# Eight gate blocks summed together in the opening of a decoder layer, x turned by products with a diagonal, second weight parts on VectorE

## The chip, the cores and the metric

The kernel runs on one core of a Trainium2 chip. Its metric is the device time of one execution in microseconds. Three runs of the kernel before gave 785.89, 786.16 and 786.79 us; the median is 786.16 us. One more execution was taken with the hardware profiler, and all lines of a trace below come from it.

## The reference

One layer of a decoder over 512 positions and 1024 channels, everything in float32. Only its beginning matters here:

```python
mod = silu(c) @ ada_w + ada_b                      # c (1, 1024), ada_w (1024, 6144)
sh1, sc1, g1, sh2, sc2, g2 = split(mod, 6)
u = rms_norm(x, mix_pre_g) * (1.0 + sc1) + sh1     # x (512, 1024)
proj = u @ w_in                                    # w_in (1024, 6152)
qk_raw, v, o_pre, gates, glu = split(proj, ...)
a, gt = split(glu, 2)                              # 1024 channels each
y = causal_dwconv(a * sigmoid(gt), cv_dw_w)        # 31 taps
y = silu(layer_norm(y))
```

Behind it stand an mLSTM over four heads (q, k, v from `proj`), an output projection, and a feed-forward part with a short convolution. A row of `mod` is a dot product of a row of `ada_w`'s transpose with `silu(c)`.

## The kernel before

**Numbers in two parts.** A float32 product that must be exact enough is made of three products: each operand is split into a first part (rounded, type `fp32r`, suffix `h` or `hi`) and a second part (what the rounding left, `l` or `lo`). `w_split` (L164) does it for weights: the first part is a copy on ScalarE (ACT) at L170, the second a subtraction at L171, on GpSimd (POOL) unless `eng` says otherwise. `mm3` (L186) issues the three products hi·hi, hi·lo, lo·hi at L188, L189 and L190.

**The gate blocks.** The columns of `w_in` that make `a` and `gt` are cut into 16 blocks of 128 columns, eight pairs. A block's result, 128 channels by 512 positions, fills one bank of PSUM, and is a sum over eight row blocks `k` of 128 channels of `u`. In the opening the first `G0 = 6` blocks (three pairs) are summed side by side, row block after row block, because the row blocks of `u` come one by one; the pairs 3 to 7 follow block by block with weights loaded by `w_load` (L174).

**The opening** (L228 to L344), in which ACT, VectorE (DVE) and POOL keep the order of the program (`in_order`, L70). TensorE (PE) and the load queue of SyncE (SP) keep program order in the whole kernel. Elsewhere a planner places the instructions of ACT, DVE and POOL by priority.

1. x is loaded in four blocks `tt` of 128 positions, each in two halves. The sum of squares of a half is made on ACT (L252) and of the other on DVE (L250); `xs` (L260) adds them and a power on POOL (L261) makes the factor of each position. DVE multiplies x by it in place (L237), and PE turns it with transposes (L232) into banks `xT`, channels on partitions. There are eight such banks `xT0` to `xT7`, but only six are free, so the transposes of 6 and 7 (L271) come when 0 and 1 are copied out by `x_out` (L277, ACT).
2. `silu(c)` is made twice, for SBUF (`cb`, L256) and in place in PSUM (`cps`, L258). `cps` holds two of the eight banks until L346.
3. For each row block `k` (L303): the load of the block's gate weights (L306), its split, the load of the next rows of `ada_w` (1 MB in two DMAs, L225), two dot products on DVE (L319, input `cps`), two small DVE instructions for scale and shift `gsk` (L322, L323), the first part of `u` on ACT (L328), the whole of it on ACT (L330), the second part on POOL (L331; on DVE for `k` = 0), and 18 products of PE. For `k` below 2 the 18 come in three passes over the banks (L338), behind that bank by bank with `mm3`.

The loads have two buffers each: a load of rows of `ada_w` waits until the dot products two blocks earlier are done, a load of gate weights until the split two blocks earlier is done.

**Behind the opening**, `glu_gate` (L350) makes `a * sigmoid(gt)` of a pair from its two banks. The 31 taps of the long convolution (L649 to L661), most of them on DVE at a low priority, need it. Their sums lie in the two banks `cv` (L97), which replace `cps`. The result is first needed by PE in `norm_mean` (L682). Behind the last tap come the dot products of later rows of `ada_w` (L155, with `cb`).

Of the kernel before, what the change touches and what calls it, by code (L numbers as in the profile page):

```python
# [17 lines left out]
P = 128  # L18
D = 1024
T = 512  # L20
# [32 lines left out]
def decoder_layer(ctx, tc, w_glu0, x, c, adaT, vecs, w_glu, w_qko, w_v0, w_v, w_out, w_up, w_down, out):  # L53
# [176 lines left out]

    def turn_x(j, tt):
        PE.transpose(xT_ps[j][:, tt * P : (tt + 1) * P], xn[tt][j // NT][:, j % NT * P : (j % NT + 1) * P], ident)  # L232

    xT_ps = [mmbank(f"xT{j}") if j % 6 < 4 else atbank(f"xT{j}") for j in range(KT)]
    def x_scale(tt, xs):
        for hf in range(2):
            V.tensor_scalar(out=xn[tt][hf], in0=xn[tt][hf], scalar1=xs[:, 1:], scalar2=None, op0=ALU.mult)  # L237
            for i in range(NT if hf == 0 else 2):
                turn_x(NT * hf + i, tt)

    opening = in_order()
    opening.__enter__()
    xss = []
    xjunks = [slot(f"xjunk{hf}") for hf in range(2)]
    for tt in range(NT):
        xsq = small.tile([P, 2], F32, tag="adap", name=f"xsq{tt}")
        for hf in range(2):
            xjunk = xjunks[hf]
            if hf:
                V.scalar_tensor_tensor(out=xjunk, in0=xn[tt][hf], scalar=1.0, in1=xn[tt][hf], op0=ALU.mult, op1=ALU.mult, accum_out=xsq[:, hf:])  # L250
            else:
                S.activation(xjunk, xn[tt][hf], AF.Square, accum_out=xsq[:, :1])  # L252
        if tt:
            x_scale(tt - 1, xss[tt - 1])
        if tt == 1:
            S.activation(cb, cps, AF.Silu)  # L256
        if tt == NT - 1:
            S.activation(cps, cps, AF.Silu)  # L258
        xs = small.tile([P, 2], F32, tag="gsk", name=f"xs{tt}")
        V.tensor_scalar(out=xs[:, :1], in0=xsq[:, :1], scalar1=xsq[:, 1:], scalar2=D * EPS, op0=ALU.add, op1=ALU.add)  # L260
        G.tensor_tensor(out=xs[:, 1:], in0=xs[:, :1], in1=mhalf[:, :1], op=ALU.pow)  # L261
        xss.append(xs)
    x_scale(NT - 1, xss[-1])

# [5 lines left out]
    xr = [slot(f"xr{j}") for j in range(KT)]  # L270
    for j in range(6, KT):  # L271
        for tt in range(NT):
            turn_x(j, tt)

# [19 lines left out]
    glu_ps = {}  # L294
    G0 = 6
    glu_w = {}
# [4 lines left out]

    banks0 = [mmbank(f"glu{i}") if i < 4 else atbank(f"glu{i}") for i in range(G0)]
    for k in range(KT):  # L303
        wk = []
        r = adas.tile([P, D], F32, tag="ada", name=f"wglu0_{k}")
        nc.sync.dma_start(r[:, : G0 * P], w_glu0[k])  # L306
        if k == 0:
            for j in range(3):
                x_out(j, S)
        for a, n in ((0, T), (T, (G0 - 4) * P)):  # L310
            wk.append(w_split(r[:, a : a + n], f"wglu0_{k}_{a}"))
        if k + 1 < KT:
# [4 lines left out]
        for i in range(2):  # L317
            junk = small.tile([P, D], BF16, tag="junk", bufs=1, name=f"junk{k}_{i}")
            V.scalar_tensor_tensor(out=junk, in0=first[k][:, i * D : (i + 1) * D], scalar=1.0, in1=cps, op0=ALU.mult, op1=ALU.mult,  # L319
                                   accum_out=part[:, i : i + 1])  # L320
# [3 lines left out]
        if k == 0:  # L324
            x_out(3, S)
            V.tensor_scalar(out=xr[0], in0=xr[0], scalar1=gsk[:, :1], scalar2=gsk[:, 1:], op0=ALU.mult, op1=ALU.add)
        hi, lo = u[k]
        S.activation(hi, xT_ps[0] if k == 0 else xr[k], AF.Identity, scale=gsk[:, :1], bias=gsk[:, 1:])  # L328
        if k:
            S.activation(xr[k], xr[k], AF.Identity, scale=gsk[:, :1], bias=gsk[:, 1:])  # L330
        (G if k else V).tensor_tensor(out=lo, in0=xr[k], in1=hi.bitcast(F32), op=ALU.subtract)  # L331
        if k == 0:
            for j in (6, 7, 4, 5):
                x_out(j, S)
        if k < 2:
            for a, b in ((0, 0), (1, 0), (0, 1)):
                for i, ps in enumerate(banks0):
                    PE.matmul(ps, blk(wk, i)[a], u[k][b], start=k == 0 and a == b, stop=False)  # L338
# [6 lines left out]
    cspool.__exit__(None, None, None)  # L345
    cvpool.append(ctx.enter_context(tc.tile_pool(name="cvpool", bufs=2, space=PSUM)))  # L346

# [797 lines left out]
def _layout(i):  # L1145
# [9 lines left out]
    def tiles(w, starts, per):  # L1155
# [22 lines left out]
    return {  # L1178
        "w_glu0": c_(np.stack([cols(w_in, a0 + b * D + j * P) for j in range(3) for b in range(2)]).transpose(2, 1, 0, 3).reshape(KT, P, 6 * P)),
        "x": c_(f("x")[0]),  # L1180
# [30 lines left out]
```

## Time and profile before

| | us |
|---|---|
| median of three runs | 786.16 |
| the profiled execution | 785.76 |
| its span, first to last instruction | 784.0 |
| PE busy in it | 762.9 |
| DVE busy | 591.6 |
| ACT busy | 408.1 |
| POOL busy | 383.9 |

A row of the timeline has the start, the duration, the engine, the line, the operation, output<-inputs, and in brackets how long the engine was idle and what ended it. PE is the matmul, PEld its load of weights, which lies beside the products. Busy time of PE includes the depth of its pipeline, so durations of neighbouring products overlap: their pace is the difference of two starts. A row of waits has the waiting engine and line, what it waited for, the sum, the number of times and the longest. A row of windows has, for each stretch, the busy time of each engine with the number of instructions, then the granted clock, the busy share of the DMA engines and their rate in GB/s.

### The profile page before, as it was taken

How to read it: one execution, taken by the hardware profiler on the slowest of the kernel's cores; microseconds unless marked ns; L12 is line 12 of the kernel's file. 1: busy time of each engine (PE TensorE's matmuls, PEld its weight loads, DVE VectorE, ACT ScalarE, POOL GpSimd, SP SyncE). 2: the span in 40 equal slices, each digit the busy share in tenths (PEclk: the TensorE clock that was granted, in tenths of full speed). 3: DMA queues.
4: the chain of work that ended last, by engine and by line, in shares of the span. 5: the costliest groups of instructions: out<-in, count | busy, mean ns of one | idle time of the engine just before them, and what ended most of it. 6: DMA issues, size and time to landing. Idle time of an engine off the chain costs nothing.

```text
span 784.0 us, 10572 instructions
## 1 busy us (share of the span) xinstructions
PE 762.9 (97%) x3683; PEld 636.5 (81%) x3683; DVE 591.6 (75%) x938; ACT 408.1 (52%) x766; POOL 383.9 (49%) x313
## 2 busy tenths in 40 slices
PE   7899999899999999999999999999999999999995
PEld 4678888678978888888888998888888888888884
DVE  6659999999998532565868798666555687698996
ACT  6566437667765544572244445444444444456752
POOL 3689758779779544334661446444544440000001
PEclk9999999999999999999999999999999999999998
DMA  8974213302116422334953763332333321778862
GB/s 292 326 274 145 93 71 108 134 28 107 54 54 234 165 89 104 114 110 155 398 176 124 253 217 135 128 123 81 120 114 128 128 91 58 279 257 259 285 222 107
DMA packets 35977, 124.28 MB, mean 159 GB/s; under 512 B 4146, under 2 KB 5586, under 8 KB 29908
## 3 DMA queue, kind: packets, MB, share of 16 engines
q1 hardware_dynamic: 24084, 95.15, 34.7%
q10 hardware_dynamic: 11840, 28.46, 10.2%
q8 instruction: 29, 0.48, 0.2%
q14 instruction: 24, 0.20, 0.1%
HBM read 112.17 MB, written 11.42 MB: 158 GB/s over the span
## 4 chain that ended last, share of the span: by engine, by line
PE 72%; DVE 17%; DMA 4%; ACT 3%; POOL 2%; issue 1%; SPq 0%; DVEq 0%; POOLq 0%; ACTq 0%
PE up L189 10%; PE up L190 10%; PE up L188 10%; DVE cv L661 8%; PE p L190 4%; PE p L189 4%; PE p L188 4%; PE glu L189 3%; DMA wglu<-in_w_glu 2%; PE glu L190 2%; PE glu L188 2%; PE mixa L190 2%; PE mixa L188 2%; PE mixa L189 2%; PE mixb L190 2%; PE mixb L189 2%
## 5 line engine op out<-in xcount | busy, mean ns | idle before, releaser
L661 DVE SCALAR_TENSOR_TENSOR cv<-gt,cvw,cv 128x506 f32<-128x506 f32 (+24 forms) x200 | 134.1, 727 | 0.4
L617 POOL TENSOR_TENSOR ro0r<-ro0t,mhalf 128x1 f32<-128x1 f32 x1 | 0.9, 926 | 125.9 <-DVE ro0t L615 125.9
L171 POOL TENSOR_TENSOR wup_1024l<-wup,wup_1024h 128x512 fp32r<-128x512 f32 x20 | 27.3, 1367 | 31.7 <-ACT wup_1024h L170 31.7
L171 POOL TENSOR_TENSOR wup_0l<-wup,wup_0h 128x512 fp32r<-128x512 f32 x20 | 27.8, 1388 | 29.9 <-ACT wup_0h L170 29.9
L657 POOL TENSOR_TENSOR cs<-cs,cs 128x510 f32<-128x510 f32 (+3 forms) x32 | 41.9, 1308 | 0.2
L171 POOL TENSOR_TENSOR wup_1536l<-wup,wup_1536h 128x512 fp32r<-128x512 f32 x20 | 28.1, 1405 | 27.4 <-ACT wup_1536h L170 27.4
L189 PE MATMUL up<-u2l,wup_0h 128*128 128x512 f32 (+1 forms) x100 | 36.5, 365 | 0.2 <-DVE u2l L830 0.2
L188 PE MATMUL up<-u2h,wup_0h 128*128 128x512 f32 (+1 forms) x100 | 36.6, 366 | 0.0
L188 PE MATMUL up<-u2h,wup_1024h 128*128 128x512 f32 (+1 forms) x100 | 36.5, 365 | 0.0
L190 PE MATMUL up<-u2h,wup_0l 128*128 128x512 f32 (+1 forms) x100 | 36.4, 364 | 0.0
L190 PE MATMUL up<-u2h,wup_512l 128*128 128x512 f32 (+1 forms) x100 | 36.4, 364 | 0.0
L190 PE MATMUL up<-u2h,wup_1536l 128*128 128x512 f32 (+1 forms) x100 | 36.4, 364 | 0.0
L188 PE MATMUL up<-u2h,wup_1536h 128*128 128x512 f32 (+1 forms) x100 | 36.4, 364 | 0.0
L189 PE MATMUL up<-u2l,wup_1024h 128*128 128x512 f32 (+1 forms) x100 | 36.4, 364 | 0.0
L189 PE MATMUL up<-u2l,wup_1536h 128*128 128x512 f32 (+1 forms) x100 | 36.4, 364 | 0.0
L188 PE MATMUL up<-u2h,wup_512h 128*128 128x512 f32 (+1 forms) x100 | 36.4, 364 | 0.0
L189 PE MATMUL up<-u2l,wup_512h 128*128 128x512 f32 (+1 forms) x100 | 36.4, 364 | 0.0
L190 PE MATMUL up<-u2h,wup_1024l 128*128 128x512 f32 (+1 forms) x100 | 36.4, 364 | 0.0
L155 DVE SCALAR_TENSOR_TENSOR junk<-ada,cb 128x1024 bf16<-128x1024 f32 x20 | 31.3, 1565 | 6.4 <-DMA ada<-in_adaT 6.2
L171 POOL TENSOR_TENSOR wup_512l<-wup,wup_512h 128x512 fp32r<-128x512 f32 x20 | 27.2, 1361 | 14.6 <-ACT wup_512h L170 14.6
L655 ACT ACTIVATE cs<-gt,cvw 128x511 f32<-128x511 f32 (+4 forms) x40 | 27.2, 712 | 4.5 <-POOL cs L657 3.8
L171 POOL TENSOR_TENSOR wqko_1024l<-wqko,wqko_1024h 128x512 fp32r<-128x512 f32 x12 | 16.6, 1382 | 22.4 <-PE v L189 12.3
(1061 smaller groups left out, 2685.1 us busy)
## 6 DMA issues: line engine op xcount, KB each, us to landing
wup<-in_w_up SPq DMA_DIRECT2D x22, 1024.0 KB, 7.0
wqko<-in_w_qko SPq DMA_DIRECT2D x12, 1024.0 KB, 5.0
ada<-in_adaT ACTq DMA_DIRECT2D x20, 512.0 KB, 5.9
ada<-in_adaT SPq DMA_DIRECT2D x16, 512.0 KB, 5.9
wo<-in_w_out SPq DMA_DIRECT2D x8, 1024.0 KB, 9.0
spare<-in_adaT ACTq DMA_DIRECT2D x12, 512.0 KB, 7.5
wglu<-in_w_glu SPq DMA_DIRECT2D x5, 1024.0 KB, 8.4
wd<-in_w_down SPq DMA_DIRECT2D x6, 768.0 KB
```

The source lines that it names most:

```text
L155: t = V.scalar_tensor_tensor(out=junk, in0=r, scalar=1.0, in1=cb, op0=ALU.mult, op1=ALU.mult, accum_out=mod[:, i : i + 1])
L171: (eng or G).tensor_tensor(out=lo[:, :n], in0=src, in1=hi[:, :n].bitcast(F32), op=ALU.subtract)
L188: PE.matmul(ps, a[0], b[0], start=start, stop=False)
L189: PE.matmul(ps, a[0], b[1], start=False, stop=False)
L190: PE.matmul(ps, a[1], b[0], start=False, stop=stop)
L617: G.tensor_tensor(out=r, in0=t, in1=mhalf[:, :1], op=ALU.pow)
L655: S.activation(t[:, d:], cvx[j][:, : T - d], AF.Copy, scale=w(CK - 1 - d))
L657: G.tensor_tensor(out=side[:, d:], in0=side[:, d:], in1=t[:, d:], op=ALU.add)
L661: last_tap = V.scalar_tensor_tensor(out=cp[:, d:], in0=cvx[j][:, : T - d], scalar=w(CK - 1 - d), in1=cp[:, d:], op0=ALU.mult, op1=ALU.add)
```

## The change

- The blocks summed together become eight (four pairs). `cps` is given back as soon as `cb` is made, and its two banks become `cv` before the opening, so that `xT` and the gate blocks each have eight banks. The second `silu(c)` goes; the dot products read `cb` in SBUF.
- x is no longer multiplied. DVE multiplies the unit matrix by the factors of the 128 positions (`dg`), and PE multiplies each block of x by this diagonal, which turns and scales in one. It is a full float32 product in place of a transpose.
- A row block's gate weights are 512 KB, loaded in one DMA, where they were 384 KB; in return one load of 1 MB behind the opening goes.
- All second parts in the opening, of the weights and of `u`, are made on DVE. In the program the split now stands behind the dot products.
- Row blocks 0 to 3 go in three passes, the others bank by bank; row block 0 takes the four banks 0 to 3 first.
- For `k` = 0 the whole of `u` is read by DVE from the bank `xT0` itself.

```diff
+    def x_sums(tt):
+        xsq = small.tile([P, 2], F32, tag="adap", name=f"xsq{tt}")
+        S.activation(xjunks[0], xn[tt][0], AF.Square, accum_out=xsq[:, :1])
+        V.scalar_tensor_tensor(out=xjunks[1], in0=xn[tt][1], scalar=1.0, in1=xn[tt][1], op0=ALU.mult, op1=ALU.mult, accum_out=xsq[:, 1:])
         xs = small.tile([P, 2], F32, tag="gsk", name=f"xs{tt}")
         V.tensor_scalar(out=xs[:, :1], in0=xsq[:, :1], scalar1=xsq[:, 1:], scalar2=D * EPS, op0=ALU.add, op1=ALU.add)
         G.tensor_tensor(out=xs[:, 1:], in0=xs[:, :1], in1=mhalf[:, :1], op=ALU.pow)
-        xss.append(xs)
-    x_scale(NT - 1, xss[-1])
+        return xs
+
+    def x_turn(tt, xs):
+        dg = slot(f"dg{tt}")[:, :P]
+        V.tensor_scalar(out=dg, in0=ident, scalar1=xs[:, 1:], scalar2=None, op0=ALU.mult)
+        for j in range(KT):
+            PE.matmul(xT_ps[j][:, tt * P : (tt + 1) * P], xn[tt][j // NT][:, j % NT * P : (j % NT + 1) * P], dg, start=True, stop=True)
+
+    xss = [x_sums(0), x_sums(1)]
+    S.activation(cb, cps, AF.Silu)
+    cspool.__exit__(None, None, None)
+    cvpool.append(ctx.enter_context(tc.tile_pool(name="cvpool", bufs=2, space=PSUM)))
+    xT_ps = [mmbank(f"xT{j}") if j < 4 else atbank(f"xT{j}") if j < 6 else cvbank(f"xT{j}") for j in range(KT)]
+    for tt in range(NT):
+        x_turn(tt, xss[tt])
+        if tt + 2 < NT:
+            xss.append(x_sums(tt + 2))
...
-    G0 = 6
+    G0 = 8
...
+    def passes(wk, k, which):
+        for a, b in ((0, 0), (1, 0), (0, 1)):
+            for i in which:
+                PE.matmul(banks0[i], blk(wk, i)[a], u[k][b], start=k == 0 and a == b, stop=False)
...
         r = adas.tile([P, D], F32, tag="ada", name=f"wglu0_{k}")
-        nc.sync.dma_start(r[:, : G0 * P], w_glu0[k])
-        if k == 0:
-            for j in range(3):
-                x_out(j, S)
-        for a, n in ((0, T), (T, (G0 - 4) * P)):
-            wk.append(w_split(r[:, a : a + n], f"wglu0_{k}_{a}"))
+        nc.sync.dma_start(r, w_glu0[k])
...
-            V.scalar_tensor_tensor(out=junk, in0=first[k][:, i * D : (i + 1) * D], scalar=1.0, in1=cps, op0=ALU.mult, op1=ALU.mult,
+            V.scalar_tensor_tensor(out=junk, in0=first[k][:, i * D : (i + 1) * D], scalar=1.0, in1=cb, op0=ALU.mult, op1=ALU.mult,
                                    accum_out=part[:, i : i + 1])
...
         if k == 0:
-            x_out(3, S)
-            V.tensor_scalar(out=xr[0], in0=xr[0], scalar1=gsk[:, :1], scalar2=gsk[:, 1:], op0=ALU.mult, op1=ALU.add)
+            for j in (1, 2, 3):
+                x_out(j, S)
+        for a in range(0, D, T):
+            wk.append(w_split(r[:, a : a + T], f"wglu0_{k}_{a}", eng=V))
         hi, lo = u[k]
-        S.activation(hi, xT_ps[0] if k == 0 else xr[k], AF.Identity, scale=gsk[:, :1], bias=gsk[:, 1:])
+        src = xr[k] if k else xT_ps[0]
+        S.activation(hi, src, AF.Identity, scale=gsk[:, :1], bias=gsk[:, 1:])
         if k:
-            S.activation(xr[k], xr[k], AF.Identity, scale=gsk[:, :1], bias=gsk[:, 1:])
-        (G if k else V).tensor_tensor(out=lo, in0=xr[k], in1=hi.bitcast(F32), op=ALU.subtract)
+            S.activation(xr[k], src, AF.Identity, scale=gsk[:, :1], bias=gsk[:, 1:])
+        else:
+            V.tensor_scalar(out=xr[k], in0=src, scalar1=gsk[:, :1], scalar2=gsk[:, 1:], op0=ALU.mult, op1=ALU.add)
+        V.tensor_tensor(out=lo, in0=xr[k], in1=hi.bitcast(F32), op=ALU.subtract)
         if k == 0:
-            for j in (6, 7, 4, 5):
+            for j in (4, 5, 6, 7):
                 x_out(j, S)
-        if k < 2:
-            for a, b in ((0, 0), (1, 0), (0, 1)):
-                for i, ps in enumerate(banks0):
-                    PE.matmul(ps, blk(wk, i)[a], u[k][b], start=k == 0 and a == b, stop=False)
+            passes(wk, k, range(4))
+            passes(wk, k, range(4, G0))
+        elif k < 4:
+            passes(wk, k, range(G0))
         else:
             for i, ps in enumerate(banks0):
                 mm3(ps, blk(wk, i), u[k], False, k == KT - 1)
```

More of the change, by code (lines that the diff above doesn't have):

```diff
@@ L229, in decoder_layer @@
     nc.sync.dma_start(vec[:, :FIRST], vecs[:, :FIRST])
[L231 to L239, printed above, removed]
     opening = in_order()
     opening.__enter__()
-    xss = []
     xjunks = [slot(f"xjunk{hf}") for hf in range(2)]
-    for tt in range(NT):
+    def x_sums(tt):
         xsq = small.tile([P, 2], F32, tag="adap", name=f"xsq{tt}")
[L247 to L258, printed above, removed]
+        S.activation(xjunks[0], xn[tt][0], AF.Square, accum_out=xsq[:, :1])
+        V.scalar_tensor_tensor(out=xjunks[1], in0=xn[tt][1], scalar=1.0, in1=xn[tt][1], op0=ALU.mult, op1=ALU.mult, accum_out=xsq[:, 1:])
         xs = small.tile([P, 2], F32, tag="gsk", name=f"xs{tt}")
@@ L300, in glu_weights @@
         glu_w[i] = w_load(w_glu[i], f"wglu{i}")
-    banks0 = [mmbank(f"glu{i}") if i < 4 else atbank(f"glu{i}") for i in range(G0)]
+    banks0 = [mmbank(f"glu{i}") if i < 4 else atbank(f"glu{i}") if i < 6 else cvbank(f"glu{i}") for i in range(G0)]
+    def passes(wk, k, which):
+        for a, b in ((0, 0), (1, 0), (0, 1)):
+            for i in which:
+                PE.matmul(banks0[i], blk(wk, i)[a], u[k][b], start=k == 0 and a == b, stop=False)
     for k in range(KT):
@@ L1178, in _layout @@
     return {
-        "w_glu0": c_(np.stack([cols(w_in, a0 + b * D + j * P) for j in range(3) for b in range(2)]).transpose(2, 1, 0, 3).reshape(KT, P, 6 * P)),
+        "w_glu0": c_(np.stack([cols(w_in, a0 + b * D + j * P) for j in range(4) for b in range(2)]).transpose(2, 1, 0, 3).reshape(KT, P, 8 * P)),
         "x": c_(f("x")[0]),
```

5 lines of the change are left out of this document (removed).

## The prediction

> **What bounds the kernel now.** I read first the windows, then what PE waited for behind the opening.
>
> ```profile
> 20.00:51.30 31.30, 28.17 (x121) 21.74 (x119) 17.96 (x42) 17.24 (x28) 22.44 (x22) 1.00 0.94 332
> 51.30:66.00 14.70, 14.70 (x65) 12.14 (x66) 11.76 (x19) 13.02 (x23) 14.19 (x12) 1.00 0.40 133
> 66.00:150.00 84.00, 84.00 (x424) 71.14 (x423) 80.26 (x131) 45.40 (x80) 68.56 (x58) 1.00 0.33 114
> ```
>
> ```profile
> PE Mb L533 <- DVE Ms L563: 2.4, 1, 2.4
> PE hT L488 <- ACT E L542: 0.4, 1, 0.4
> PE up L189 <- DVE u2l L830: 0.2, 1, 0.2
> ```
>
> From 51.3 us to the tail PE waits three times, 3.0 us in all: PE is the bound there, and an earlier end of the opening should reach the end of the kernel. Between 20 and 51 us the DMA engines are 94% busy at 332 GB/s and PE issues only 121 products, though their pace would allow more:
>
> ```profile
> ACT wglu_0h L170 <- DMA wglu<-in_w_glu: 11.8, 6, 3.3
> DVE junk L319 <- DMA ada<-in_adaT: 9.3, 7, 2.9
> PE glu L189 <- POOL ul L331: 3.1, 3, 1.4
> 65.97 0.39 PE L190 MATMUL glu<-uh,wglu_1536l 128*128 128x512 f32 x1
> 66.19 0.39 PE L188 MATMUL glu<-uh,wglu_0h 128*128 128x512 f32 x1
> 17.20 1.48 PE L338 MATMUL glu<-uh,wglu_0h 128*128 128x512 f32 x4 [0.49 <-ACT uh L328]
> ```
>
> A product takes 0.227 us (65.97 to 66.19). The first is issued at 17.20, and the eighth block ends where the ninth begins, at 66.19: 49.0 us for 192 products that need 192 x 0.227 = 43.6. So **5.4 us of waiting for loads and splits** is what can be won; the change fills it with the fourth pair. The point to follow is this 66.19.
>
> **The turn of x.** It needs the four factors. The last block's square ends at 10.28 on ACT and its power is short:
>
> ```profile
> 9.56 0.63 ACT L252 ACTIVATE xjunk<-xn 128x512 f32<-128x512 f32 x1 [0.72 <-DMA xn<-in_x]
> 10.10 0.18 ACT L252 ACTIVATION_READ_ACCUMULATOR xjunk<-xn 128x1 f32 x1
> 11.67 0.21 DVE L260 TENSOR_SCALAR xs<-xsq 128x1 f32<-128x1 f32 x1
> L261 POOL TENSOR_TENSOR xs<-xs,mhalf x4: 551/924/932, 5.8 to 12.0; 128x1 f32<-128x1 f32 x4
> L237 DVE TENSOR_SCALAR xn<-xn,xs x8: 479/484/487, 6.8 to 12.9; 128x512 f32<-128x512 f32 x8
> ```
>
> Today DVE reaches the last sum at 11.67, behind 0.88 us of scaling per block. With a 128x128 diagonal (between L266's 0.17 and L237's 0.48; I take 0.24, near the small one, since a quarter of L237's elements is left) the sum comes at about 10.4, the power ends at 11.5 to 11.7, the last diagonal at 11.9. The first diagonal is there at about 7.4, where the transposes begin now; PE has work from then on without a gap, and its pace decides:
>
> ```profile
> 15.65 0.23 PEld L232 LDWEIGHTS xT<-ident,xn 128*128 128x128 f32 x1
> 15.86 0.23 PEld L232 LDWEIGHTS xT<-ident,xn 128*128 128x128 f32 x1
> L232 PE MATMUL xT<-ident,xn x32: 417/421/477, 7.3 to 16.3; 128*128 128x128 f32 x32
> L488 PE MATMUL hT<-ident,hn x32: 270/273/329, 211.6 to 363.7; 128*128 128x128 f32 x32
> 333.06 1.06 PE L203 MATMUL ry_b<-ident,ry_r 128*128 128x128 f32 x8
> 333.87 0.48 PE L188 MATMUL mixa<-wo_512h,hh 128*128 128x512 f32 x1
> L139 PE MATMUL cps<-crow,ones x4: 1056/1056/1189, 2.4 to 5.1; 1*128 1x512 f32 x4
> ```
>
> A transpose is one record and a float32 product two (L203: eight records for four products, 0.81 us to the next row, 0.10 each). In the opening records come 0.21 us apart and last 0.42 us, against 0.27 us for L488's later: **PE is at half speed to the end of the transposes**, though the windows say 1.00 there. So a product with the diagonal costs 0.43 us at half speed and 0.20 at full; 32 are 13.8 or 6.4 us. When does the speed rise? After an idle time it is seen once:
>
> ```profile
> 154.16 0.77 PE L533 MATMUL Mb<-Ms,rowsel 128*128 128x512 f32 x1 [2.38 <-DVE Ms L563]
> 154.73 0.63 PE L188 MATMUL qko<-uh,wqko_1024h 128*128 128x512 f32 x1
> 155.16 0.63 PE L189 MATMUL qko<-ul,wqko_1024h 128*128 128x512 f32 x1
> 157.16 0.40 PE L188 MATMUL qko<-uh,wqko_1024h 128*128 128x512 f32 x1
> ```
>
> After 2.4 us of idleness products are 0.43 us apart, and 3.0 us of dense work bring the full pace back; the loss is about 1.3 us. At the start of the program it took longer: transposes with gaps of 0.5 us from 7.3 did it at about 16.5, the four one-row products of L139, dense from 2.4 to 6, not at all. For dense full products from 7.4 I take the rise at 12.0 (4.6 us), between 3.0 us and 9. By then 10.7 products are done; 21.3 x 0.20 = 4.3 us more: the turn ends at 16.3 instead of 16.7, its last eight begin at 14.7.
>
> The Trainium skill, "TensorE: Matmul & The Clock Gate", Part 1, says that the clock is full after a busy window of about 3.4 us that runs freely; by it the rise would fall between 10.8 and 14.2, an estimate that leaves my 12.0 inside. Its Part 4 says that transposes do not count as work for the clock; here the first gate products behind them are at full speed already (L338's weight loads last 0.19 us from 17.2 on), so the trace does not bear that out.
>
> **To the first gate product.**
>
> ```profile
> 13.60 1.57 ACT L277 ACTIVATE xr<-xT 128x512 f32<-128x512 f32 x3 [2.41 <-PE xT L232]
> 15.05 0.64 ACT L170 ACTIVATE wglu_0h<-wglu 128x512 fp32r<-128x512 f32 x1
> L927 DVE TENSOR_TENSOR g2l<-g2kept,g2h 128x512 fp32r<-128x512 f32 x11 | 7.5, 682 | 0.0
> 16.39 0.93 DVE L326 TENSOR_SCALAR xr<-xr,gsk 128x512 f32<-128x512 f32 x1
> ```
>
> On ACT three copies (0.48 each, 13.60 to 15.05) now stand ahead of the first split, and the third bank's turn allows the first at 15.3: split at 16.74, done at 17.37. DVE makes two second parts, which begin at 17.45 and take 0.65 of pace each (0.68 by L927, with POOL idle), and then the whole of `u` for `k` = 0 out of `xT0`, 0.7 to 0.93 (0.7 taken). Block 0's sum uses that bank, so the first gate product waits for this: 18.75 + 0.7 + 0.1 = **19.55**, 2.35 us later than now. PE idles there 3.2 us (16.3 to 19.55), more than the 2.4 that cost the full speed at 154; I take the same 1.3 us loss, between 0 and 1.5. The dot products of block 0, from about 12 with `ada` landed, are done before; the second `silu` that goes (1.0 us of ACT) stood beside transposes and is worth nothing.
>
> **Per row block.** PE needs 24 x 0.227 = 5.45 us.
>
> ```profile
> 18.38 1.21 DVE L319 SCALAR_TENSOR_TENSOR junk<-ada,cps 128x1024 bf16<-128x1024 f32 x1
> 21.09 1.21 DVE L319 SCALAR_TENSOR_TENSOR junk<-ada,cps 128x1024 bf16<-128x1024 f32 x1
> 21.27 0.82 ACT L328 ACTIVATE uh<-xr,gsk 128x512 fp32r<-128x512 f32 x1 [1.35 <-DVE gsk L323]
> 22.12 0.82 ACT L330 ACTIVATE xr<-xr,gsk 128x512 f32<-128x512 f32 x1
> L319 DVE SCALAR_TENSOR_TENSOR junk<-ada,cps x16: 1207/1220/1222, 13.5 to 46.3; 128x1024 bf16<-128x1024 f32 x16
> L155 DVE SCALAR_TENSOR_TENSOR junk<-ada,cb x20: 1209/1438/2318, 235.9 to 471.3; 128x1024 bf16<-128x1024 f32 x20
> ```
>
> DVE: dot products and `gsk` 2.71 (18.38 to 21.09), two second parts to 4.0, then it waits for ACT, which ends the whole of `u` at 0.18 + 1.67 behind `gsk`, 4.56; `ul` to **5.3**. The new wait sits on DVE: the next block's dot products are queued behind `ul`, and with them the release of the `ada` buffers to SP. DMA: 1.57 MB at 332 GB/s is 4.74 us, and a load has about 8 us from its release to its use (two periods less the 2.6 of the dot products). The 1 MB that goes behind the opening stood in a stretch with 40% of DMA and is worth nothing there; nor is the order of the passes, since PE has its operands either way. So the order is PE 5.45, DVE 5.3, DMA 4.74: PE sets the pace, with `ul` of `k` = 0 at 20.1 and of `k` = 7 at 20.1 + 37.1 = 57.2, ahead of its use at 59.0.
>
> The dot products' second input moves from PSUM to SBUF. L155 has that form: 1.21 us at best, 2.3 at worst, in stretches where POOL works. I take 1.22, since POOL has only the factors to make here.
>
> The Trainium skill, "VectorE: DVE Perf Modes", "Two Vector instructions with no wait between them", says that the second SBUF read of VectorE is shared with GpSimd. By it the new form would be the worse one beside a busy POOL; with 2.3 us twice a row block would take 7.5 us. L155's spread fits the rule.
>
> **Sum.** 19.55 + 1.3 + 43.6 = 64.45 against 66.19: **1.7 us won**. The profiled execution (785.76, span 784.0) would be 784.0; it lies 0.4 below the median, and against the median 786.16 I say **784.4**. This is 0.22%, at the edge of what a measurement of this kernel tells from no change (0.2%, 1.6 us).
>
> **What is late next.** All four pairs end together, and the taps' bank is the fourth pair's: the first tap moves from 55.5 to about 66.
>
> ```profile
> L661 DVE SCALAR_TENSOR_TENSOR cv<-gt,cvw,cv x200: 706/726/750, 55.5 to 235.3; 128x502 f32<-128x502 f32 x6, 128x506 f32<-128x506 f32 x5, 128x504 f32<-128x504 f32 x5, 128x489 f32<-128x489 f32 x5
> 311.87 1.02 PE L682 MATMUL ytot<-ysum,ones 128*128 128x512 f32 x2
> ```
>
> DVE did some 15 taps (10 us) by then and is full afterwards, so the last tap goes from 235 to 242 to 246. PE asks for the result at 312: hidden, by 50 us of cover. The dot products of L155 behind it move to 246 to 275.
>
> **Rivals.**
> - *The clock stays down* (slower): products of a diagonal, mostly zeros, raise the speed no better than L139's. The turn ends at 7.4 + 13.8 = 21.2, the first gate product follows at 23.0, the end at 67.9: 787.9. Each us by which the rise comes later costs 0.53 us, so it decides from a rise at about 15.3. For it: nine slow us today. Against it: 3.0 us sufficed at 154. Chance 0.25.
> - *The speed is kept over the gap*, or rises by 10.5: 63.15, or 62.4 with both: 783.1 to 782.4. For it: gaps of 1.3 us cost nothing between 26 and 52. Against it: 154. Chance 0.18.
> - *Given back on DVE*: L155's instructions, 1.2 to 2.3 us each, now stand before `Md` and `E` of the next head, for which PE waits 0.4 us at 266.8 already. One such delay: 785.6 to 786.7; with several on the path 788. Chance 0.16.
> - *The round trip of DVE and ACT, or the larger loads, become the bound*: from 5.56 us per block it shows, at 5.8 nothing is won: 786.1 and above. Against it: the sums above. Chance 0.08.
>
> **Chances.** The forecast itself has 0.33; half of it and a bit lies beyond 0.2%. With the second rival: faster 0.42. The rest of the forecast, part of the first and third: same 0.33. Slower 0.25, mostly the first rival. The range 782.3 to 788.2 reaches from the kept clock to the clock that stays down.
>
> **What would show it.** PE records of the turn falling from 0.21 to 0.10 us apart at about 12; the first L338 successor near 19.5 with products 0.43 apart for some 3 us; dot products of two blocks 5.3 to 5.5 us apart; the ninth block's first product near 64.5; no new wait of PE behind it. Wrong would be a first gate product behind 21.3, DVE waiting for `ada` loads, or a new wait of PE between 240 and 280.

## The result and the profile after

The change makes the kernel **slower**: 789.32 us (787.99 to 789.57, five runs) against 786.10 (785.37 to 786.79, five runs), a ratio of 1.0041 with a 95% interval of 1.0029 to 1.0052. A second set gave 1.0038 (1.0023 to 1.0053). Two executions of over 2700 us, the profiled one of e13 below and one of the kernel before beside e9 to e12, are left out of the ratios, and e13's trace is not read. The profiled execution took 787.99 us, 2.2 more than that of before; its span is 786.2 against 784.0. The trace is of the fastest of the five runs, 1.3 us below their median.

First the opening, in TensorE's timeline of the changed kernel. L250 is the product with the diagonal, L301 the first gate product, L188 at 64.82 the ninth block's first:

```profile
7.73 9.29 PE L250 MATMUL xT<-dg,xn 128*128 128x128 f32 x64 [1.76 <-DVE dg L248]
19.05 1.37 PE L301 MATMUL glu<-uh,wglu_0h 128*128 128x512 f32 x4 [2.02 <-ACT uh L326]
...
64.82 0.39 PE L188 MATMUL glu<-uh,wglu_0h 128*128 128x512 f32 x1
```

The point that the prediction followed stands at 64.82 instead of 66.19: the opening wins 1.37 us. Then what TensorE waits for in the whole kernel (sum, times, longest):

```profile
PE hT L486 <- DVE hn L480: 4.0, 1, 4.0
...
PE glu L301 <- ACT uh L326: 2.0, 1, 2.0
...
PE glu L189 <- DVE ul L331: 1.3, 1, 1.3
PE Mb L531 <- DVE Ms L561: 0.6, 1, 0.6
```

The first row is new. `hT` turns the result of a head and waits for `hn`, its normalized form; this wait is that of head 1. The lead of 1.37 us grows at `Mb` of head 0 (a wait of 0.6 us, and no half clock behind it, where before had 2.4 and the half clock) and is lost at that `hT`. Before, then after, in TensorE's timeline of 250 to 274 us:

```profile
256.89 0.40 PE L533 MATMUL Mb<-Ms,rowsel 128*128 128x512 f32 x1
266.77 0.66 PE L488 MATMUL hT<-ident,hn 128*128 128x128 f32 x4 [0.42 <-ACT E L542]
270.14 1.02 PE L455 MATMUL s<-q_0c,k_2c 128*128 128x512 f32 x2
```

```profile
253.38 0.40 PE L531 MATMUL Mb<-Ms,rowsel 128*128 128x512 f32 x1
266.42 2.03 PE L486 MATMUL hT<-ident,hn 128*128 128x128 f32 x8 [4.02 <-DVE hn L480]
270.81 0.41 PE L188 MATMUL v<-wv_4h,uh 128*128 128x256 f32 x1
271.02 0.33 PE L189 MATMUL v<-wv_4l,uh 128*128 128x256 f32 x1
272.13 0.28 PE L189 MATMUL v<-wv_5l,uh 128*128 128x256 f32 x1
272.25 0.28 PE L190 MATMUL v<-wv_5h,ul 128*128 128x256 f32 x1
272.38 1.02 PE L453 MATMUL s<-q_0c,k_2c 128*128 128x512 f32 x2
```

At `Mb` of head 2 the changed kernel is 3.51 us ahead, at `s` of head 2 2.24 us behind, which is the difference of the spans. Of the 5.75 us, 4.02 are the wait, against 0.42 before; the other 2.15 are lost behind it, mostly because products come 0.21 us apart until 271.0 (270.81 to 271.02) and 0.12 from then on (272.13 to 272.25): the idle time cost the full speed. The windows 262 to 273 show it, before and then after (granted clock third from the end):

```profile
262.00:273.00 11.00, 10.58 (x74) 8.98 (x72) 4.94 (x8) 9.26 (x20) 5.26 (x4) 1.00 0.17 59
```

```profile
262.00:273.00 11.00, 6.98 (x38) 6.38 (x37) 9.83 (x17) 4.38 (x8) 8.16 (x6) 0.69 0.53 179
```

DVE is busy 9.8 of these 11 us where it had been 4.9, and DMA 53% where it had been 17%. The chain of waits of the changed kernel, 250 to 275 us, says with what:

```profile
255.16 0.04 DVE cv L659
...
255.79 1.81 DVE junk L155 x2
...
257.62 0.33 ACTq L153
...
257.98 1.28 ACT L538
...
260.00 3.68 DMA ada<-in_adaT
...
263.77 1.23 DVE junk L155 x2
265.01 1.28 DVE hn L480
```

Behind the last tap (L659, the `cv` row) come dot products of the rows 16 to 23 (L155). Their loads (L153) are issued in ACT's order, each when a dot product has freed one of the two buffers; DVE waits for the load, and `hn` waits behind both, until 265.0. GpSimd had its factor `fac` ready 2.9 us before, at 262.10:

```profile
261.07 1.03 POOL L477 TENSOR_TENSOR fac<-ssq,mhalf 128x4 f32<-128x4 f32 x1
```

In the kernel before the taps had ended 20 us earlier. The taps' group, after (first and last start at the end of the figures):

```profile
L659 DVE SCALAR_TENSOR_TENSOR cv<-gt,cvw,cv x200: 691/726/750, 69.6 to 255.2; 128x483 f32<-128x483 f32 x7, 128x498 f32<-128x498 f32 x5, 128x489 f32<-128x489 f32 x5, 128x487 f32<-128x487 f32 x5
```

### The profile page after: what moved, and what is told of

Read it like the earlier page. It is cut to its first block, busy times and chain, and to the rows that moved or that the text cites. A ratio compares the mean times of both kernels' runs of the same rounds, so it can differ in the third digit from the quotient of the medians.

```text
span 786.2 us, 10624 instructions
## 1 busy us (share of the span) xinstructions
PE 763.6 (97%) x3715; PEld 640.9 (82%) x3715; DVE 606.2 (77%) x957; ACT 406.0 (52%) x760; POOL 353.9 (45%) x286
## 4 chain that ended last, share of the span: by engine, by line
PE 72%; DVE 20%; ACT 3%; DMA 2%; issue 1%; SPq 0%; ACTq 0%; DVEq 0%
PE up L189 10%; PE up L190 10%; PE up L188 10%; DVE cv L659 9%; PE p L189 4%; PE p L190 4%; PE p L188 4%; PE glu L189 2%; PE glu L190 2%; PE glu L188 2%; DVE junk L314 2%; PE mixa L190 2%; PE mixa L188 2%; PE mixa L189 2%; PE mixb L190 2%; PE mixb L189 2%
## 5 line engine op out<-in xcount | busy, mean ns | idle before, releaser
L659 DVE SCALAR_TENSOR_TENSOR cv<-gt,cvw,cv 128x497 f32<-128x497 f32 (+24 forms) x200 | 135.7, 727 | 1.6 <-ACT cv L647 0.9
L188 PE MATMUL up<-u2h,wup_0h 128*128 128x512 f32 (+1 forms) x100 | 36.5, 365 | 0.0
L188 PE MATMUL up<-u2h,wup_1024h 128*128 128x512 f32 (+1 forms) x100 | 36.4, 364 | 0.0
L188 PE MATMUL up<-u2h,wup_512h 128*128 128x512 f32 (+1 forms) x100 | 36.4, 364 | 0.0
L188 PE MATMUL up<-u2h,wup_1536h 128*128 128x512 f32 (+1 forms) x100 | 36.4, 364 | 0.0
L155 DVE SCALAR_TENSOR_TENSOR junk<-ada,cb 128x1024 bf16<-128x1024 f32 x20 | 30.6, 1530 | 7.4 <-DMA ada<-in_adaT 7.3
L170 ACT ACTIVATE wup_1024h<-wup 128x512 fp32r<-128x512 f32 x22 | 13.9, 631 | 25.9 <-PE up L189 20.4
```

Of the source, the lines that this page charges most:

```text
L155: t = V.scalar_tensor_tensor(out=junk, in0=r, scalar=1.0, in1=cb, op0=ALU.mult, op1=ALU.mult, accum_out=mod[:, i : i + 1])
L170: S.activation(hi[:, :n], src, AF.Copy)
L188: PE.matmul(ps, a[0], b[0], start=start, stop=False)
L659: last_tap = V.scalar_tensor_tensor(out=cp[:, d:], in0=cvx[j][:, : T - d], scalar=w(CK - 1 - d), in1=cp[:, d:], op0=ALU.mult, op1=ALU.add)
```

## The experiments

Each ratio is against the kernel before on the same chip; the changed kernel itself was run beside e5 to e7 only, so the other runs are set beside it by their ratios. **Theory**: the four pairs end together, so the taps start and end later; the dot products and loads of rows 16 to 23, which follow the last tap, then stand in front of `hn` of head 1. **Rivals**: GpSimd's backlog makes `hn`'s factor late; or the new opening itself loses the time.

| run | median us | ratio, 95% interval |
|---|---|---|
| the change again | 788.88 | 1.0038 (1.0023 to 1.0053) |
| e1 rows 16 to 23 later | 786.48 | 1.0026 (1.0010 to 1.0042) |
| e2 the same in before | 786.38 | 1.0002 (0.9984 to 1.0021) |
| e3 first split of the fifth pair later | 790.10 | 1.0061 (1.0048 to 1.0074) |
| e4 both | 788.03 | 1.0040 (1.0023 to 1.0058) |
| e5 before, taps later | 788.70 | 1.0038 (1.0023 to 1.0053) |
| e6 eight taps fewer on DVE | 788.22 | 1.0031 (1.0014 to 1.0047) |
| e7 transposes for the diagonal | 786.12 | 1.0003 (0.9986 to 1.0020) |
| e9 loads of rows 16 to 23 on SP | 787.27 | 1.0023 (1.0013 to 1.0032) |
| e10 e7 and e1, loads on SP | 784.93 | 0.9993 (0.9983 to 1.0004) |
| e11 e7, loads on SP | 784.70 | 0.9985 (0.9970 to 1.0001) |
| e12 before, loads on SP | 791.81 | 1.0082 (1.0068 to 1.0096) |
| e13 e7, rows behind head 2 | 811.23 | 1.0318 (1.0300 to 1.0336) |
| e15 the same with the diagonal | 810.29 | 1.0301 (1.0282 to 1.0320) |
| e14 e7, rows before the gates | 801.68 | 1.0211 (1.0190 to 1.0231) |
| e8 before, second parts on DVE | 807.23 | 1.0269 (1.0243 to 1.0296) |
| e16 e7, rows beside the gates | 788.10 | 1.0030 (1.0016 to 1.0045) |
| e17 the same with the diagonal | 788.04 | 1.0032 (1.0015 to 1.0049) |

**The dot products behind another point (e1, e2).**

```diff
     for i in range(16, 24):
-        ada_block(i, last_tap)
+        ada_block(i, los[1])      # head 1's last second part (L492)
```

> The changed kernel with the eight dot products of rows of ada_w behind the last tap (L155, blocks 16 to 23) placed behind the last second part of head 1's attention instead. Theory A (these dot products and their loads stand in front of hn on VectorE and hold PE 4.0 us at hT, and the idle time costs the full clock, 1.3 us more): the wait falls to 0.5 us or less, nothing runs at half speed behind it, and the time goes from 789.3 to 784 to 785. Theory B (the late taps have filled GpSimd, and the factor fac, which ended at 262.1, is late by itself): the wait stays at 1.2 to 2.2 us and the time is 786.5 to 788. If neither is it: 789.

> The same placement in the kernel before, as a control. Theory A: only the 0.4 us wait of PE at hT can go: 785.6 to 786.3, no change clear of noise. If the placement is worth something by itself, without the changed opening: 784 or below.

TensorE's waits in e1:

```profile
PE o L464 <- ACT hn L468: 3.1, 1, 3.1
...
PE hT L486 <- DVE hn L480: 0.5, 1, 0.5
```

The wait at `hT` falls from 4.0 to 0.5 us, so these dot products did stand in its way; but 30 us later, in the same attention step of head 2, ACT comes late with a copy, and TensorE waits 3.1 us. ACT had waited for buffers of L155:

```profile
290.85 0.63 ACT L170 ACTIVATE wv_4h<-wv 128x512 fp32r<-128x512 f32 x1 [2.28 <-DVE junk L155]
```

Then, at 293.62, ACT waited 2.14 us more for `q_1c`, which DVE made late behind such a dot product. So the wait moved. The forecast of 784 to 785 us was missed, though the traced execution, of 784.49 us, lies in it: by the ratios about a third of the loss came back, but the intervals overlap (1.0010 to 1.0042 against 1.0029 to 1.0052). In the kernel before the same edit makes a wait of 2.2 us at `o` and no gain: it is no improvement of its own.

**The hiccup at the end of the opening (e3, e4).** In the changed kernel ACT splits the fifth pair's weights between `uh` and `xr` of row block 7, which makes the 1.3 us at `ul`. e3 moves the call of the fifth pair's `w_load` into the ordered part, behind row block 7; e4 adds e1.

```diff
+    glu_weights(G0 // 2)
     opening.__exit__(None, None, None)
...
-        glu_weights(i)
+        if i > G0 // 2:
+            glu_weights(i)
```

> The changed kernel with the split of the fifth pair's weights kept behind the opening's last instruction on ScalarE (in the changed kernel its first piece, waiting for its load, stands in front of the whole of u of the last row block and holds PE 1.25 us at ul). The ninth block begins 1.3 us earlier, at 63.5. Theory A or B (hn is set by other engines, not by PE): PE then waits at hT longer by as much, and the time stays at 789 (788.5 to 789.5). If PE's lead is kept instead: 788.0.

> Both edits together. Theory A: 782.7 to 784, since the 1.3 us of the opening now reach the end. Theory B: 786 to 787.5, the opening's 1.3 us are lost at hT. Neither: 788 to 789.

The wait at `ul` goes in both, and the time does not: e3's waits at `Mb` and `hT` are 1.8 and 2.8 us (the latter in two). But its ninth block also begins later, at 65.13 instead of the 63.5 expected: TensorE's clock rose later in that run, and the first gate products ran at half speed behind their wait of 2.03 us (last section). In e4 it is 65.51. So neither says what 1.3 us won in the opening would be worth, and e4's 788.03 is the value expected if neither theory holds.

**The change again, and late taps alone (e5).**

> The changed kernel itself, beside the three that follow. Both theories: 1.0030 to 1.0052 of the kernel before, TensorE idle about 4.0 us at hT of head 1 (262 to 266 us), ninth block's first product near 64.8 us. A profile near 789.5 us instead of 788.0 would show one more stretch at half clock; theory: behind the wait at Mb of head 0 (140 to 160 us) or behind the gap at 17 to 20 us.

e5 is the kernel before, whose first taps wait for the fourth pair's gate:

```diff
+            if j < 3 and d == SIDE + 1:
+                tc.add_manual_dep(last_tap.ins, gates[3].ins.name, ...)
```

> The kernel before with one thing alone taken from the changed one: the taps on VectorE begin only behind the fourth pair's gate (near 67 us instead of 55.5). The opening is that of before, so the ninth block's first product stays at 66.2 us. Theory A (late taps push the adaLN dot products of rows 16 to 23 in front of hn): last tap 245 to 250 us instead of 235, TensorE idle 1.5 to 4 us at hT of head 1 near 262 us, time 1 to 4 us above the kernel before. Rival (the new opening itself, its PSUM or its splits, makes the loss): last tap moves, but the wait at hT stays 0 and the time is within 0.7 us of before.

The first taps of the first three pairs wait so. The taps' group in e5, then TensorE at its longest wait behind the opening, and a row of its waits:

```profile
L662 DVE SCALAR_TENSOR_TENSOR cv<-gt,cvw,cv x200: 689/725/750, 67.6 to 253.6; 128x506 f32<-128x506 f32 x6, 128x498 f32<-128x498 f32 x6, 128x504 f32<-128x504 f32 x5, 128x502 f32<-128x502 f32 x5
```

```profile
210.38 1.46 PE L489 MATMUL hT<-ident,hn 128*128 128x128 f32 x8 [2.43 <-DVE hn L483]
```

```profile
PE s L456 <- DVE E L457: 1.4, 2, 1.0
```

With before's opening untouched (its ninth block begins at 66.17), starting the taps 12 us later ends them 18 us later and costs the same 0.4% as the whole change. **So the late taps cost time by themselves, and the new opening is not needed for it.** The place is not the expected one. The wait at `hT` is that of head 0, at 210 us, where DVE does eight taps in a row ahead of `hn`; no dot product of rows 16 to 23 has come by then. At head 1, near 262 us, TensorE does not wait. Behind it those dot products stand in front of `E` of head 2 (the 1.4 us at `s`), as the prediction's third rival said. Two things stay open. The trace is of an execution of 786.64 us, 2.1 below e5's median, and shows a loss of 0.9 us only. And e5 has no wait at `Mb` of head 0 either (TensorE is there at 151.66, before at 154.16): what the changed kernel wins there can come from the late taps alone, without its opening.

**Fewer taps on DVE (e6).** `SIDE = 6`: eight taps go to ACT and POOL.

> The changed kernel with SIDE = 6: one tap in each of eight pairs goes from VectorE (8 x 0.73 us less there) to ScalarE and GpSimd (8 x 1.3 us more there). Theory A (VectorE is late): last tap near 249 us instead of 255, the wait at hT falls from 4.0 to 2 us or less, time 1 to 2 us below the changed kernel on the same chip. Theory B (GpSimd's backlog makes fac late): the wait at hT stays at 4 us or grows, time equal or up to 3 us above the changed kernel.

```profile
PE s L453 <- DVE so L488: 3.2, 1, 3.2
...
PE hT L486 <- DVE hn L480: 0.8, 1, 0.8
```

The last tap starts at 245.0, the wait at `hT` falls to 0.8, as the theory said and GpSimd's rival did not. But `so`, one link further in the same chain, now waits behind a dot product whose load is late, and the time is within the interval of the changed kernel's. The theory had the place right and the gain wrong. `hn` itself now waits 2.2 us for GpSimd's factor (3.7 in e9): that backlog is next in line, at under 1 us for TensorE at head 1, and not the cause.

**Transposes instead of the diagonal (e7).** DVE scales x and TensorE turns it with transposes; banks, order and second parts stay as in the changed kernel.

```diff
-        dg = slot(f"dg{tt}")[:, :P]
-        V.tensor_scalar(out=dg, in0=ident, scalar1=xs[:, 1:], scalar2=None, op0=ALU.mult)
...
+            V.tensor_scalar(out=xn[tt][hf], in0=xn[tt][hf], scalar1=xs[:, 1:], scalar2=None, op0=ALU.mult)
...
+                PE.transpose(xT_ps[j][:, tt * P : (tt + 1) * P], xn[tt][hf][:, j % NT * P : (j % NT + 1) * P], ident)
```

> The changed kernel with the diagonal part alone undone: x is scaled on VectorE and turned by transposes into the same eight banks. TensorE's clock then rises only in the gate products. Forecast: first gate product 17 to 18 us instead of 19.05, 1.3 to 2 us lost at half clock behind it, so the ninth block's first product within 0.8 us of 64.8. If the end is set by VectorE's late taps at 255 to 265 us, the time is within 0.7 us of the changed kernel either way; if the opening's lead carries through, it moves by what the ninth block moves.

```profile
8.15 6.64 PE L250 MATMUL xT<-ident,xn 128*128 128x128 f32 x32 [2.00 <-DVE xn L248]
17.35 1.91 PE L301 MATMUL glu<-uh,wglu_0h 128*128 128x512 f32 x4 [2.57 <-ACT uh L326]
...
62.90 0.39 PE L188 MATMUL glu<-uh,wglu_0h 128*128 128x512 f32 x1
```

32 records in 6.64 us at half speed instead of 64 in 9.29. The ninth block begins at 62.90, 1.9 us ahead of the changed kernel's, and the time is 2.8 us less (786.12 against 788.88, same chip): the opening's lead does reach the end, less the price of the late taps (its wait at `hT` is 4.4 us). That was the second branch of the expectation; its ninth block, within 0.8 us of 64.8, was missed. **The diagonal is a loss**, and e9 and e11 below, which differ in it alone, say the same: 787.27 against 784.70 us.

As an estimate from the medians, the late taps cost 3.0 us in e5, 3.7 in e7 (a lead of 3.3 at the ninth block becomes a loss of 0.4) and 4.5 in the changed kernel (a lead of 1.3 becomes a loss of 3.2): alike, and not the same.

**The loads of rows 16 to 23 on SP's queue (e9 to e12).** e9 is the changed kernel, e11 e7, e10 e7 with e1's edit, e12 the kernel before, each with

```diff
-        nc.scalar.dma_start(r, adaT[i // 2]...)
+        (nc.sync if i < 24 else nc.scalar).dma_start(r, adaT[i // 2]...)
```

> The changed kernel with the loads of adaLN rows 16 to 23 issued from SyncE's queue instead of ScalarE's; the planner then puts their dot products later in VectorE's order (behind the hn of heads 1 and 2). Theory (late taps bring those dot products, and loads that wait in ScalarE's order, in front of hn and the attention's own copies): the wait at hT of head 1 falls from 4.0 to under 1 us, no wait of 3 us at o as in the first experiment, the half-clock stretch at 262 to 271 us goes, time 2 to 4 us below the changed kernel (0.9975 to 1.0015 of the kernel before). Rival (the six late taps and GpSimd's backlog are enough by themselves): hT still waits 2 us or more, time within 1 us of the changed kernel.

> Transposes instead of the diagonal, the dot products of rows 16 to 23 behind head 1's last second part, and their loads on SyncE's queue. Theory: the ninth block's first product at 63 us (3.2 us ahead of the kernel before) and no wait over 1 us until 330 us, so the lead stays: 0.995 to 0.998 of the kernel before. Rival (the lead is given back wherever VectorE is late): 0.999 to 1.002.

> Transposes instead of the diagonal and the loads of rows 16 to 23 on SyncE's queue, dot products where the planner puts them. Theory: as the one before, 0.995 to 0.998 of the kernel before; a remaining wait at hT is put down to GpSimd's fac. Rival: 0.999 to 1.002.

> The kernel before with the loads of rows 16 to 23 on SyncE's queue, to see what that edit is worth by itself. In the kernel before hT waits 0.4 us, so theory: within 1 us of the kernel before (0.9985 to 1.001). If it gains 2 us or more, the gain of the three others is not the recovered lead but this edit.

In e9 the dot products come after 282 us. The wait at `hT` of head 1 falls to under 0.5, and another comes at head 2's:

```profile
PE hT L486 <- ACT E L540: 2.4, 1, 2.4
...
PE ry_s L196 <- DVE so L488: 0.9, 1, 0.9
PE hT L486 <- DVE hn L480: 0.6, 2, 0.4
```

e9 is 0.0015 below the changed kernel, less than forecast, and the intervals overlap. e10 and e11 begin the ninth block at 62.52 and 62.16 and have the same wait at head 2; at 0.9993 and 0.9985 they are the best of the study, level with the kernel before, where 0.995 to 0.998 was forecast. For e11 the interval (0.9970 to 1.0001) leaves open whether it is ahead of it. In the kernel before the edit costs 0.8% (e12; within 1 us was forecast), with waits of 2.4 and 1.3 us at `hT`, so their standing is not that edit's own gain.

**Loads put ahead of weights (e13, e14, e15), and one part alone (e8).** e13 and e15 put the dot products behind head 2's last second part, e14 in front of the gates; loads on SP.

> Transposes instead of the diagonal; the dot products of rows 16 to 23 behind head 2's last second part (beyond 320 us, where VectorE is busy about half of the time), their loads on SyncE's queue. Theory (these dot products are what stands in front of the attention's work wherever VectorE is late): no wait of 2 us or more of TensorE between 70 and 330 us, ninth block's first product near 62.9 us, 0.994 to 0.997 of the kernel before. Rival (VectorE and GpSimd are late by themselves, the dot products only share it): hT waits 2 us or more somewhere, 0.998 to 1.002.

> The changed kernel (with the diagonal) with the dot products of rows 16 to 23 behind head 2's last second part, loads on SyncE's queue. Theory: it stands behind the same with transposes by what the ninth block stands behind (about 1.9 us): 0.9965 to 0.9995 of the kernel before, and 2.5 to 5 us ahead of the changed kernel. Rival (the diagonal's cost is hidden): equal to the one with transposes within 0.7 us.

> Transposes instead of the diagonal; the dot products of rows 16 to 23 go to the start of the gates (55 to 75 us), where VectorE waits about 7 us for gates, loads on SyncE's queue. Theory: taps end 2 to 8 us later than in the changed kernel (257 to 263 us) but nothing stands in front of hn of head 1 except taps, so hT of head 1 waits under 1.5 us; 0.994 to 0.998 of the kernel before. Rival (any work that is late on VectorE at 255 to 265 us delays hn, taps too): hT waits 2 us or more, 0.999 to 1.003. A wait of the glu products on their weights near 58 to 75 us would show the loads collide.

Waits of TensorE in e15, then e14:

```profile
PE mixa L188 <- ACT wo_0h L170: 23.7, 1, 23.7
```

```profile
PE glu L188 <- ACT wglu_0h L170: 16.4, 1, 16.4
```

These three failed as tests. The loads wait on SP for one of two buffers, weights stand behind them, and TensorE waits 16.4 us in e14 and 23.7 in e15. Neither theory nor rival is judged by them.

e8 is the kernel before with the second parts of its opening on DVE:

```diff
-            wk.append(w_split(r[:, a : a + n], f"wglu0_{k}_{a}"))
+            wk.append(w_split(r[:, a : a + n], f"wglu0_{k}_{a}", eng=V))
...
-        (G if k else V).tensor_tensor(out=lo, in0=xr[k], in1=hi.bitcast(F32), op=ALU.subtract)
+        V.tensor_tensor(out=lo, in0=xr[k], in1=hi.bitcast(F32), op=ALU.subtract)
```

> The kernel before with the second parts of its opening on VectorE alone: this part alone, the opening's order, banks and transposes as before. It adds 25 or so halves of 0.69 us to VectorE before 60 us and takes away the three waits for GpSimd's ul (3.1 us). Theory: the waits for ul shorten by 1 to 3 us, taps still start near 55.5 us, last tap 235 to 240 us, so no wait over 1 us at hT of head 1: 0.996 to 1.000 of the kernel before. Rival (the second parts on VectorE are what makes the taps late): last tap beyond 245 us and a wait at hT, 1.002 or more.

```profile
PE glu L338 <- ACT uh L328: 6.2, 2, 4.4
PE glu L189 <- DVE ul L331: 5.8, 5, 1.6
PE glu L188 <- ACT uh L328: 3.4, 4, 1.7
```

My expectation was far off. This part alone costs 2.7%. TensorE waits in nearly each row block, and late in the opening the blocks come 6.1 us apart (its waits at `ul` end at 54.75 and 60.83), while the 18 products of three pairs are 4.1 us by the 0.227 us of one. That three pairs have too few products to cover the longer round trip of DVE and ACT, and four enough, is the likely reason, and was not tested apart. The signs that the expectation named for its rival are there too (last tap at 253.1, a wait of 1.3 us at `hT` of head 0), but TensorE is by then 17 us late from the opening.

**The dot products beside the gates (e16, e17).** They follow the opening's last second part; the loads are on SP, and a pair's weights stand ahead of its four loads.

```diff
         glu_weights(i)
+        for n in range(4 * i, 4 * i + 4):
+            if n < 24:
+                ada_block(n, opened)
```

> Transposes instead of the diagonal; dot products of rows 16 to 23 behind the opening's last second part on VectorE, four of them with the fifth pair, four with the sixth, so that the weights of a pair stand ahead of its four loads on SyncE's queue; the loads of rows 24 and on stay where they were. Theory (dot products of rows 16 to 23 and their loads are what turns late taps into waits): no wait for wglu over 3 us, taps end 256 to 264 us, hT of head 1 waits under 1.5 us, 0.994 to 0.998 of the kernel before. Rival (late work on VectorE, taps too, delays hn): hT waits 2 us or more, 0.999 to 1.003. If the loads still hold up the weights (a wait of 5 us or more at glu), neither is tested and the time is above 1.004.

> The same with the diagonal of the changed kernel. Theory (the diagonal's price is paid in full once nothing else waits): 1.5 to 3 us behind the one with transposes, 0.997 to 1.001 of the kernel before. Rival (the price is hidden in a later wait): within 0.7 us of the one with transposes.

e16's taps, and its largest wait:

```profile
L664 DVE SCALAR_TENSOR_TENSOR cv<-gt,cvw,cv x200: 707/725/752, 70.4 to 267.1; 128x506 f32<-128x506 f32 x6, 128x502 f32<-128x502 f32 x6, 128x504 f32<-128x504 f32 x5, 128x500 f32<-128x500 f32 x5
```

```profile
PE aT L561 <- DVE ga L556: 4.3, 1, 4.3
```

The taps end 12 us later still, and no wait at `hT` is left in either kernel: at head 1 the taps alone do not delay `hn`, the dot products and loads did (at head 0 of e5 taps alone did). But DVE is busy nearly all of the time from 80 to 260 us, and the wait comes back at 149 us, where `ga`, a link of head 0's decay, comes late between the taps and TensorE waits 4.3 us. The weights wait too (1.8 us at 87 us in e17). Neither reached its forecast (0.994 to 0.998 and 0.997 to 1.001). The two are equal, so the diagonal's price is not seen between them: e17's clock rose early, its ninth block began at 63.33 against 62.81, and its wait at `aT` is 0.6 us.

## Why the prediction was wrong

Forecast 784.4 us, measured 789.32. By its own steps:

- *The turn of x*: right in its mechanism. The rise of the clock was taken at 12.0 us and came at 11.7, as the windows of one us show (TensorE's records of L250 in brackets); the turn ends at 17.02 (16.3 taken). But the step compared the diagonal with the transposes of the kernel before, which end at 16.7, and not with transposes into the eight new banks: those end at 14.8 (e7). So it took for a gain of 0.4 us what is a loss.

```profile
10.70:11.70 1.00, 1.00 (x6) 1.00 (x6) 1.00 1.04 404
11.70:12.70 1.00, 1.00 (x11) 1.00 (x10) 1.00 1.03 416
```

- *First gate product* 19.55: it came at 19.05. *The loss of 1.3 us behind the gap* was not there: the gap was 2.02 us and the full speed was kept in this run (in e3 and e4, with a gap of 2.03, it was not). Instead 1.3 us were lost at `ul` of row block 7, an order of the planner at the end of the opening that the prediction did not see.
- *Per row block*: right. DVE's period was 5.15 us (5.3), a dot product 1.22 (1.22), and between the first gate product and `ul` of row block 7 no wait of TensorE is listed.
- *Ninth block's first product* 64.45: it came at 64.82, with two errors of 1.3 us against each other. That the sum fits is luck; the second trace of this kernel has 64.87, those of the other runs with the diagonal 63.33 to 65.51.
- *What is late next*: **this step failed.** "The last tap goes from 235 to 242 to 246", "hidden, by 50 us of cover". It went to 255, by 20 us. The cover was looked up for the taps' result (needed at 312), where it holds; the dot products behind the taps on DVE, and their loads in ACT's order, stand in front of `hn` of head 1, for which TensorE was ready at 262.4: a wait of 4.02 us and 2.15 us behind it, where the prediction had put nothing. Late taps alone cost the kernel before 3.0 us (e5), if at other places.
- *What bounds the kernel* failed with it: "PE is the bound there, and an earlier end of the opening should reach the end". DVE, at 80.26 of 84 us in the row quoted for it, was nearly as full, and what TensorE won it lost where DVE was late.
- The start of the taps slipped by 14 us, since the gates of the first pairs are at 63 instead of 53, and DVE waits for them: between 55 and 66 us it is busy for 3.26 us, where it had been for 10.86. The other 6 us were not taken apart. From 80 us to the last tap DVE is busy for 97.7% of the time in the kernel before and 98.5% in the changed one, so what isn't done early is done at the end.
- *The rival "given back on DVE"* had mechanism and place (L155 in front of the next head's work, and "a new wait of PE between 240 and 280" as the sign). Its price was too low: 785.6 to 786.7 for one delay; the delay was 4.0 us with 2.15 us behind it, because the speed fell. Its chance of 0.16 was small for a window with DVE at 80.26 of 84 us.
- *The clock stays down*, the prediction's main danger, did not come in any run with the diagonal; the latest rise was at about 14.0 us (e4).

The sum of the trace: 1.4 us won at the ninth block, 2.1 more by 253 us (mostly at `Mb` of head 0), 5.75 lost at `hT` and behind it. The diagonal's share of the opening, 1.9 us between the ninth blocks of this kernel and of e7, is a further cost.

Open: why runs of the changed kernel lie near 788.0 and near 789.5, 1.5 us apart (no trace of one near 789.5 was taken; the half speed behind the first gap and behind `Mb` in e3's trace, of 789.82 us, is a candidate), how the cost of the late taps in e5 is spread, and whether e11 is ahead of the kernel before.

## What to carry to other kernels

Where an engine off the critical path is as full as DVE here (80.26 of 84 us), moving the start of its work moves its end, and whatever is queued behind that end; look for cover at everything behind it on that engine, not only at its own consumer. A wait moved from there (e1, e6, e16) mostly comes back further on, so judge it by the time, not by the row that vanished. A wait of TensorE can cost more than itself: the one of 4.02 us here cost 2.15 more. And before a trace explains a loss, see whether its execution has that loss: e5's has under a third of it.

## What the runs showed of the hardware

- **The rise of TensorE's clock varies from run to run.** In the turn by diagonals, dense from its start, the pace of records doubled at about 10.7 us (e17, start 7.64), 11.7 (after, 7.73) and 13.2 (e3, 7.90): 3.1 to 5.3 us behind the start. In e4 (start 7.90) it was later still, at about 14.0. The windows of one us, e3:

```profile
11.70:12.70 1.00, 1.00 (x6) 1.00 (x6) 1.00 1.02 415
12.70:13.70 1.00, 1.00 (x9) 1.00 (x8) 1.00 1.03 422
13.70:14.70 1.00, 1.00 (x12) 1.00 (x11) 1.00 1.03 422
```

  The granted clock reads 1.00 throughout: in the first 16 us the pace of records shows the speed, the column does not. The Trainium skill, "TensorE: Matmul & The Clock Gate", Part 1, says that the window is free-running and that the transition varies by 0.5 us to either side. No run here shows the window itself; the spread of the three, 2.2 us behind the start, is wider than that. The ninth block begins at 63.33 in e17 and at 65.13 in e3; their edits differ too, so the clock's share is not taken apart.
- **The length of an idle time alone does not decide whether TensorE keeps its speed.** The same gap ahead of the first gate products, 2.02 us after and 2.03 in e3, kept it after (products 0.23 us apart from 20.25 us on) and dropped it in e3 (0.43 apart; granted clock 0.50 from 20.9 to 22.9). The same wait of 2.38 us at `hT` of head 2 dropped it in e10 and kept it in e11. The longest gap that kept it is e1's at `o`, with a granted clock of 1.00 before and after. Gaps from 1.64 (e17, `Mb`) to 4.02 us (after, `hT`) dropped it. e3, then e1:

```profile
19.87 1.92 PE L301 MATMUL glu<-uh,wglu_0h 128*128 128x512 f32 x4 [2.03 <-ACT uh L326]
```

```profile
295.82 1.57 PE L464 MATMUL o<-v,E 128*128 128x258 f32 x6 [3.06 <-ACT hn L468]
```

- **A DMA issue that waits for a buffer stops the engine whose order it stands in**: ACT for 2.28 us in e1's row above, and SP in e14, whose order the eight loads of such rows hold from 48.1 to 71.0 us; the gate weights are issued behind them, at 71.08, and TensorE waits 16.4 us for them.
